# One more output tile kept in PSUM in the dense expert stage, and gates stored two first keys at a time

## The chip, the cores and the metric

The kernel runs on one core of a Trainium2 chip. The metric is the device time of one execution in microseconds. The engines are TensorE (PE, its weight loads PEld), VectorE (DVE), ScalarE (ACT), GpSimd (POOL), which here only issues gathers, and SyncE (SP), which issues all other DMAs.

## The reference

A decoder block on 1,024 tokens of width 1,024: RWKV-7 mixing beside differential attention, a gated merge, then a PEER layer of 16,384 experts, and a last RMSNorm. Only the PEER layer is touched by the change:

```python
q = (hf @ w_q).reshape(T, 8, 2, 128)
s = einsum('thcd,hcnd->thcn', q, sub_keys)      # 128 first keys, 128 second keys
v1, i1 = top_k(s[:, :, 0], 16); v2, i2 = top_k(s[:, :, 1], 16)
vals, ci = top_k((v1[..., :, None] + v2[..., None, :]).reshape(T, 8, 256), 16)
ids = first_key * 128 + second_key              # 8 x 16 experts of each token
gates = softmax(vals)
act = gelu(einsum('ced,cd->ce', u_tab[ids], x)) * gates
y = einsum('ce,ced->cd', act, v_tab[ids])
```

## The kernel before

The PEER layer is computed in two ways at the same time. Four blocks of 128 tokens take the **gather** way (`peer`, L809): for each of the 128 choices POOL gathers one row of `u`, and later one of `v`, for each token (128 x 1,024 floats, 512 KB, into one of NU = 5 buffers `uv`), and DVE does one instruction over 128x1024 on it (L817 for `u`, L824 for `v`). That makes 1,024 gathers and 1,024 long DVE instructions. A gather can start when DVE is done with the buffer that it takes.

The other 512 tokens take the **dense** way (`dense`, L864): all 16,384 experts as matrix products, one first key `e` (128 experts) at a time, with gates of 0 for the experts that a token did not choose. `head(e)` loads two tiles of `ut`, splits them in an upper and a lower part (`whi` on ACT, `wlo` on DVE), makes the dots with 24 matmuls in a PSUM bank `ua` of the pair `zbank` (L854), reads it out through Gelu on ACT (L886), multiplies by the gates on DVE (`gw`, L887), splits the result (`ah` on ACT, `al` on DVE), and loads and splits two tiles of `v` (`vh`, `vl`). Then each of eight output tiles (4 blocks of tokens x 2 halves of the width) gets three matmuls for this key. For e under NE = 16 the dots come from DRAM (`a_s`), where they were put during the gate stage.

PSUM has eight banks: `zbank` 2, `rbank` 3, `abank` 2, `obank` 1. Six of the output tiles are kept (`yk`) in the last three kinds for all 128 keys. The other two are moved: at every second key (CV = 2) `rest` (L902) makes the products of two keys, six matmuls, in a bank `yr` of `zbank`, and DVE adds it to `accd` in SBUF (L907). MV says ahead of which kept tile each `rest` stands: 0 and 3. The two `zbank`s go round over the dots and the two moved tiles.

The gate stage (`gates`, L827) comes just ahead. For 32 tokens at a time it builds gates in `st`, laid out as [second key, first key / CE, token, first key % CE], and writes them to DRAM (`gd_s`, L850). `dense` reads them back as `gt` (L882), CE = 4 first keys at a time, 512 tokens x 4 floats on a partition, in two buffers. So L887 reads one float of each group of four. At the end `finish` (L799) normalises each block: its square sums, the weight `fnw` loaded into a tile with the tag of `gt`, and the last product L806.

The order of the instructions on each engine is fixed before the run by the tile framework's planner. It goes by a clock of its own with its own costs: when an engine is free on that clock, the instruction that is ready and stands first in the program goes next. `dense` stands ahead of `peer` in the program, so its DVE instructions go first and the gathers' instructions fill what is left. On the chip each engine then runs its list strictly in order.

Of the kernel before, what the change touches and what calls it, by code (L numbers as in the profile page):

```python
# [8 lines left out]
F32 = mybir.dt.float32  # L9
# [9 lines left out]
P = 128  # L19
# [16 lines left out]
NE = 16  # L36
MV = (0, 3)
CHO = (1, 1, 1, 1, 0)
PADB = 8 * (16 * P + 16)
CE = 4  # L40
CV = 2
# [4 lines left out]
def body(ctx: ExitStack, tc: tile.TileContext, ins, out, dbg=None):  # L46
# [44 lines left out]

# [1 line left out]
    def const(name, shape, dt=F32):  # L93
# [57 lines left out]
    def wmul(o, src, xh, xl, n=8, step=1):  # L151
        """o = the sum over n [128, 128] parts of a weight tile src [n / 4, 128, 512], transposed, times xh(k) + xl(k).

        The lower parts of the weights come after the upper ones of step parts."""
        w = []
        for k0 in range(0, n, step):
            ks = range(k0, k0 + step)
            for k in ks:
                if k % 4 == 0:
                    w.append(wsplit(src[k // 4]))  # L160
                hi = w[-1][0][:, (k % 4) * P:(k % 4 + 1) * P]
                nc.tensor.matmul(o, hi, xh(k), start=(k == 0), stop=False)  # L162
                nc.tensor.matmul(o, hi, xl(k), start=False, stop=False)  # L163
            for k in ks:
                lo = w[k // 4][1][:, (k % 4) * P:(k % 4 + 1) * P]
                nc.tensor.matmul(o, lo, xh(k), start=False, stop=(k == n - 1))  # L166
# [10 lines left out]
    def invroot(ssq, n, scale, eps, op1=OP.add, pool=None):  # L177
        """(ssq * scale + eps) ** -0.5 for [128, n] (op1 max: the larger of the two)."""
        w = (pool or hp).tile([P, 32], F32, name="rsw", bufs=2)
        x, y, t, xh = (w[:, 8 * i:8 * i + n] for i in range(4))  # L180
        nc.vector.tensor_scalar(x, ssq, scale, eps, op0=OP.mult, op1=op1)
        nc.vector.tensor_scalar(xh, x, -0.5, None, op0=OP.mult)
        # a first guess from the exponent, then Newton's steps
        nc.vector.tensor_single_scalar(y.bitcast(U32), x.bitcast(U32), 1, op=OP.logical_shift_right)
        nc.vector.tensor_scalar(y.bitcast(U32), y.bitcast(U32), -1.0, 1597463007.0, op0=OP.mult, op1=OP.add)
        for _ in range(3):
            nc.vector.tensor_tensor(t, y, y, op=OP.mult)
            nc.vector.tensor_tensor(t, t, xh, op=OP.mult)
            nc.vector.scalar_tensor_tensor(y, t, 1.5, y, op0=OP.add, op1=OP.mult)
        return y  # L190
# [9 lines left out]
    def normed(src, w):  # L200
        """RMSNorm of rows of src, w over all partitions (two halves [128, 512] each)."""
        xn = [rt("xn") for _ in HALVES]
        ssq = tiny("ssq", 2)
        for i in range(2):
            nc.scalar.activation(xn[i], src[i], AF.Square, accum_out=ssq[:, i:i + 1])
        nc.vector.tensor_tensor(ssq[:, 0:1], ssq[:, 0:1], ssq[:, 1:2], op=OP.add)
        r = invroot(ssq[:, 0:1], 1, 1.0 / D, 1e-6)
        for i in range(2):
            nc.vector.scalar_tensor_tensor(xn[i], src[i], r[:, 0:1], w[i], op0=OP.mult, op1=OP.mult)
        return xn  # L210

    def to_cols(xn, a, hi, lo):
        """Rows of 128 tokens (two halves) to the transposed hi, lo [128, column / 128, token]."""
        o = slice(a * P, (a + 1) * P)
        for i in range(2):
            b = abank("tr")
            for k in range(4):
                nc.tensor.transpose(b[:, k * P:(k + 1) * P], xn[i][:, k * P:(k + 1) * P], ident)
            ks = slice(4 * i, 4 * i + 4)
            nc.scalar.activation(hi[:, ks, o], v4(b), AF.Copy)  # L220
            nc.vector.tensor_tensor(lo[:, ks, o], v4(b), hi[:, ks, o].bitcast(F32), op=OP.subtract)

    def head_stats(sq, W, scale, eps, op1):
        """Per token and half of the partitions: (sum(sq) * scale, eps) ** -0.5, spread back over them."""
        n = W // P
# [4 lines left out]
        o = rbank("hb")  # L230
# [7 lines left out]
    def mix(gi, t0, W):  # L238
# [27 lines left out]

# [1 line left out]
        c3 = lambda ap: ap.rearrange("p (c s) -> p c s", s=CH)  # L268
# [5 lines left out]
        def rwkv(h, kz, rz, vz):  # L274
# [46 lines left out]

            # A matrices, all transposed ([s, t]) and block diagonal over the chunks
            MB = [[None] * TT, [None] * TT]
# [36 lines left out]

            # (1 + A)^-1: blocks of 16 by substitution, a block to a partition, then doubling
            ab = gp.tile([64, 16, 16], F32, name="ab16", bufs=1)
# [73 lines left out]
            Pd, Qm = [], []  # L436
            # the state after a chunk is G * (Pd S + Qm): Pd with the 1, G already in Qm; off the heads' blocks 0
            def block(name, b, x, op):
# [67 lines left out]

# [1 line left out]
        def att_in(h):  # L508
# [20 lines left out]
        def attention(h, qT, kT, vn):  # L529
# [9 lines left out]
            for a in range(TT):  # L539
# [24 lines left out]
                if t0:  # L564
                    # the sums divide in the transposes: products with diagonal matrices
                    dg = at("dg")
# [61 lines left out]

# [1 line left out]
        yh, yl, mcat = [], [], []  # L630
# [50 lines left out]
    def pick(t0, W, fh, fl):  # L681
        """PEER: queries, keys, choice."""
        TT = W // P
# [30 lines left out]
    def choose(v1, i1, bi, last):  # L714
        """The 16 best sums of the two lists of each head: ids and gates [128, 128]."""
        cand = t4("cand")[:, :8 * NCAND].rearrange("p (h j) -> p h j", h=8)
# [23 lines left out]
        nc.vector.tensor_tensor(g3, g3, gsum[:, :, None].to_broadcast([P, 8, 16]), op=OP.mult)  # L740
        # position -> (i, j): the regions of REG hold 2^4, 2^3, 2^2, 2^1 columns
        d1, d2 = at("d1"), at("d2")
# [11 lines left out]
        nc.vector.tensor_tensor(fj, pf, ir, op=OP.subtract)  # L754
        # first row of a region less its first position >> its shift: 0, -2, -8, -24
        nc.vector.scalar_tensor_tensor(g1, h2, 2.5, g1, op0=OP.mult, op1=OP.add)
# [21 lines left out]
        if last:  # L778
            # with the choices over the partitions
            b = abank("sl")  # L780
# [18 lines left out]
    def finish(acc, rows, pool, tag, bufs):  # L799
        """The last norm of acc [128, 1024], and out."""  # L800
        ssq = pool.tile([P, 1], F32, name="ssqf", bufs=2)
# [7 lines left out]
    def peer(bi, ids, gate):  # L809
        """The chosen experts of 128 tokens, a choice at a time by gathers."""  # L810
        rows = slice(bi * P, (bi + 1) * P)
# [15 lines left out]
    def gates(sp, a, sl, eye8):  # L827
        """Gates [first key / CE, second key, token, first key % CE]: sums of outer products of one-hot rows."""
        e1, g = sl[:, 0:P], sl[:, 2 * P:3 * P]
# [27 lines left out]
    def ahead(sp, W, fh, fl, es):  # L857
        """The products with the rows of u of the first keys es, to a_s."""
        for e in es:
            t = sp.tile([P, 512], F32, name="ue", bufs=2)[:, :W]  # L860
            nc.scalar.activation(t, dots(e, W, fh, fl), AF.Copy)
            nc.sync.dma_start(ins["a_s"][e, :, 0:W], t)

    def dense(t0, W, fh, fl):  # L864
        """The experts of W tokens as matrix products over all of them, with gates of 0 for those not chosen."""
        TT = W // P
# [5 lines left out]
        outs = [(a, 0) for a in range(TT)] + [(a, 1) for a in range(TT)][::-1]  # L872
        banks = (rbank, rbank, rbank, obank, abank, abank)
        kept = {o: f("yk") for o, f in zip(outs, banks)}
# [3 lines left out]
        def head(e):  # L878
            """For the experts of first key e: weights (hi, lo: [128 second keys, W]), rows of v (hi, lo by halves)."""
            if e % CE == 0:  # L880
                gt[0] = fp.tile([P, 512, CE], F32, name="gt", bufs=2)
                nc.sync.dma_start(gt[0][:, :W], ins["gd_s"][e // CE, :, 0:W, :])  # L882
# [39 lines left out]
        for a in range(TT):  # L922
            for h in range(2):
                if (a, h) in kept:
                    y = acc[a][:, HALVES[h]]
                    nc.vector.tensor_tensor(y, y, kept[a, h], op=OP.add)
            finish(acc[a], slice(t0 + a * P, t0 + (a + 1) * P), fp, "gt", 2)

# [29 lines left out]
def prepare(inputs):  # L958
# [5 lines left out]
    a["x"] = c(g["x"].reshape(T, D))  # L964
    # [column tile, half of the rows, 128 rows, 4 row tiles x 128 columns]
    wt = lambda w: c(w.reshape(2, 4, P, -1, P).transpose(3, 0, 2, 1, 4).reshape(-1, 2, P, 512))
# [16 lines left out]
    a["lora"] = c(np.stack([np.concatenate([g["w2"][0], g["a2"][0]], axis=0), g["g2"][0]], axis=1))  # L983
    # constants of the shapes
    a["ident"] = np.eye(P, dtype=f)
# [45 lines left out]
```

## Time and profile before

| | |
|---|---|
| median of 3 runs | 3668.87 us (3668.75 to 3677.71) |
| profiled execution, span from first to last instruction | 3659.9 us |
| the median less that span (what lies around it) | 9.0 us |
| PE busy, DVE busy, ACT busy, POOL busy | 88%, 82%, 37%, 37% |
| DMA, mean over the span | 247 GB/s |

For the profiled execution its span is what is shown; a change in the span is taken as a change in the time. Busy shares are over the whole span, and the stages differ: from about 2290 to 3600 us PE, DVE and the DMA engines are all above nine tenths.

### The profile page before, as it was taken

How to read it: one execution, taken by the hardware profiler on the slowest of the kernel's cores; microseconds unless marked ns; L12 is line 12 of the kernel's file. 1: busy time of each engine (PE TensorE's matmuls, PEld its weight loads, DVE VectorE, ACT ScalarE, POOL GpSimd, SP SyncE). 2: the span in 40 equal slices, each digit the busy share in tenths (PEclk: the TensorE clock that was granted, in tenths of full speed). 3: DMA queues.
4: the chain of work that ended last, by engine and by line, in shares of the span. 5: the costliest groups of instructions: out<-in, count | busy, mean ns of one | idle time of the engine just before them, and what ended most of it. 6: DMA issues, size and time to landing. Idle time of an engine off the chain costs nothing. (4 is left out here: it accounts for less than half of the span.)

```text
span 3659.9 us, 46805 instructions
## 1 busy us (share of the span) xinstructions
PE 3224.0 (88%) x15166; PEld 2571.2 (70%) x15166; DVE 2995.0 (82%) x6666; ACT 1344.7 (37%) x2497; POOL 1350.5 (37%) x1100
## 2 busy tenths in 40 slices
PE   6999989998979796678888868999999999999997
PEld 5878867776857675556665656777777777777775
DVE  4655555978889888899988758998999999999997
ACT  3333433343323342122498863322222332222332
POOL 0000000004454445552012223656566665565652
PEclk9988989997979897788989879999999999999998
DMA  4222234426676667886467888999999999999995
GB/s 138 62 72 76 73 109 152 135 79 221 226 239 231 229 235 271 314 319 207 125 207 225 263 282 316 348 340 351 349 356 351 350 351 345 347 340 352 348 351 184
DMA packets 407110, 903.24 MB, mean 247 GB/s; under 512 B 52240, under 2 KB 139088, under 8 KB 402768
## 3 DMA queue, kind: packets, MB, share of 16 engines
q0 software_dynamic: 147456, 536.94, 41.6%
q1 hardware_dynamic: 259408, 363.31, 29.3%
q8 instruction: 119, 1.95, 0.2%
q14 instruction: 127, 1.04, 0.1%
HBM read 831.41 MB, written 68.69 MB: 246 GB/s over the span
## 5 line engine op out<-in xcount | busy, mean ns | idle before, releaser
L795 POOL DMA_INDIRECT uv<-u,ids x512 | 656.7, 1283 | 1140.4 <-DVE uv L817 538.3
L795 POOL DMA_INDIRECT uv<-v,ids x512 | 673.0, 1315 | 582.4 <-DVE acc L824 416.0
L824 DVE SCALAR_TENSOR_TENSOR acc<-uv,act,acc 128x1024 f32<-128x1024 f32 x512 | 655.9, 1281 | 52.4 <-DMA uv<-v,ids 46.0
L817 DVE SCALAR_TENSOR_TENSOR uv<-uv,hb 128x1024 f32<-128x1024 f32 x512 | 617.3, 1219 | 78.2 <-DMA uv<-u,ids 77.2
L147 ACT ACTIVATE whi<-wraw 128x512 fp32r<-128x512 f32 x552 | 344.7, 630 | 741.8 <-PE z L163 252.7
L162 PE MATMUL ua<-fh,whi 128*128 128x512 f32 x1024 | 428.7, 419 | 83.4 <-DVE accd L907 68.2
L148 DVE TENSOR_TENSOR wlo<-wraw,whi 128x512 fp32r<-128x512 f32 x552 | 373.7, 686 | 155.0 <-ACT whi L147 151.3
L163 PE MATMUL ua<-fl,whi 128*128 128x512 f32 x1024 | 422.6, 413 | 0.0
L173 PE MATMUL yk<-vh,ah 128*128 128x512 f32 x768 | 304.3, 396 | 21.7 <-ACT ah L169 20.8
L174 PE MATMUL yk<-vl,ah 128*128 128x512 f32 x768 | 304.3, 396 | 10.8 <-DVE vl L170 10.8
L162 PEld LDWEIGHTS ua<-fh,whi 128*128 128x128 f32 x1024 | 204.5, 200 | 147.5 <-DVE accd L907 85.9
L169 ACT ACTIVATE ah<-gw 128x512 fp32r<-128x512 f32 x128 | 80.8, 631 | 614.0 <-DVE gw L887 614.0
L175 PE MATMUL yk<-vh,al 128*128 128x512 f32 x768 | 304.0, 396 | 0.0
L162 PE MATMUL z<-hh,whi 128*128 128x512 f32 x672 | 273.8, 408 | 1.5 <-ACT whi L147 0.9
L166 PE MATMUL ua<-fh,wlo 128*128 128x512 f32 x1024 | 266.6, 400 | 5.3 <-DVE wlo L148 5.3
L166 PE MATMUL z<-hh,wlo 128*128 128x512 f32 x672 | 270.7, 403 | 0.0
L163 PE MATMUL z<-hl,whi 128*128 128x512 f32 x672 | 270.0, 402 | 0.0
L846 PE MATMUL gb<-oh,ohg 128*128 128x128 f32 x1024 | 226.4, 342 | 40.5 <-ACT ohg L845 39.1
L846 PEld LDWEIGHTS gb<-oh,ohg 128*128 128x128 f32 x1024 | 166.1, 209 | 103.8 <-ACT ohg L845 66.5
L163 PEld LDWEIGHTS ua<-fl,whi 128*128 128x128 f32 x1024 | 204.4, 200 | 44.6
L166 PEld LDWEIGHTS ua<-fh,wlo 128*128 128x128 f32 x1024 | 195.0, 191 | 48.5 <-DVE wlo L148 5.8
L845 ACT ACTIVATE ohg<-ohb,sl 128x128 f32<-128x128 bf16 x512 | 228.1, 537 | 2.5 <-DVE ohb L840 2.4
(325 smaller groups left out, 6199.0 us busy)
## 6 DMA issues: line engine op xcount, KB each, us to landing
wraw<-ut SPq DMA_DIRECT2D x256, 256.0 KB, 6.4
vraw<-v SPq DMA_DIRECT2D x256, 256.0 KB, 6.5
wraw<-w_in SPq DMA_DIRECT2D x168, 256.0 KB, 2.7
gd_s<-st SPq DMA_DIRECT2D x16, 2048.0 KB, 11.2
gt<-gd_s SPq DMA_DIRECT2D x32, 1024.0 KB, 8.9
wraw<-wq SPq DMA_DIRECT2D x64, 256.0 KB, 2.9
g_s<-sgo SPq DMA_DIRECT2D x32, 256.0 KB, 3.1
wraw<-proj SPq DMA_DIRECT2D x32, 256.0 KB, 3.6
```

The lines of the kernel that those rows point to most:

```text
L147: nc.scalar.activation(hi, raw, AF.Copy)
L148: nc.vector.tensor_tensor(lo, raw, hi.bitcast(F32), op=OP.subtract)
L162: nc.tensor.matmul(o, hi, xh(k), start=(k == 0), stop=False)
L163: nc.tensor.matmul(o, hi, xl(k), start=False, stop=False)
L166: nc.tensor.matmul(o, lo, xh(k), start=False, stop=(k == n - 1))
L173: nc.tensor.matmul(o, ah, bh, start=first, stop=False)
L174: nc.tensor.matmul(o, ah, bl, start=False, stop=False)
L175: nc.tensor.matmul(o, al, bh, start=False, stop=last)
L795: nc.gpsimd.indirect_dma_start(out=t, out_offset=None, in_=ins[src], in_offset=bass.IndirectOffsetOnAxis(ap=ids[:, j:j + 1], axis=0))
L817: nc.vector.scalar_tensor_tensor(u, u, 1.0, hb, op0=OP.mult, op1=OP.mult, accum_out=act[:, j:j + 1])
L824: nc.vector.scalar_tensor_tensor(acc, v, act[:, j:j + 1], acc, op0=OP.mult, op1=OP.add)
L846: nc.tensor.matmul(b[:, k * P:(k + 1) * P], o3[:, k], o1[:, k], start=True, stop=True)
```

## The change

Seven output tiles are kept instead of six; the seventh takes one of the two `zbank`s. One tile is left to be moved, and its `rest` stands ahead of the third kept tile (MV = (2,)). The dots of all keys and this tile now share the one `zbank` that is left. CE goes from 4 to 2: `gd_s` is [64, 128, 512, 2] instead of [32, 128, 512, 4], `st` and `gt` follow, and `gt` has three buffers of half the size, which `finish` uses too. Comments and docstrings are dropped.

```diff
-MV = (0, 3)
+MV = (2,)
-CE = 4
+CE = 2
 def dense(t0, W, fh, fl):
-        banks = (rbank, rbank, rbank, obank, abank, abank)
+        banks = (rbank, rbank, rbank, obank, abank, abank, zbank)
 def head(e):
             if e % CE == 0:
-                gt[0] = fp.tile([P, 512, CE], F32, name="gt", bufs=2)
+                gt[0] = fp.tile([P, 512, CE], F32, name="gt", bufs=3)
                 nc.sync.dma_start(gt[0][:, :W], ins["gd_s"][e // CE, :, 0:W, :])
...
-            finish(acc[a], slice(t0 + a * P, t0 + (a + 1) * P), fp, "gt", 2)
+            finish(acc[a], slice(t0 + a * P, t0 + (a + 1) * P), fp, "gt", 3)
```

## Rows read from the trace of the kernel before

**Rows 1.** Busy time by stretch: PE, PEld, DVE, ACT, POOL, PEclk, DMA share, GB/s

```profile
1760.00:2180.00 420.00, 337.09 (x1490) 252.35 (x1488) 330.40 (x885) 330.89 (x723) 88.79 (x76) 0.89 0.70 219
2180.00:2289.00 109.00, 97.06 (x399) 75.28 (x400) 94.93 (x114) 39.25 (x69) 40.36 (x31) 0.98 0.89 322
2289.00:3604.40 1315.40, 1245.77 (x5221) 995.20 (x5220) 1227.81 (x1641) 382.33 (x659) 787.29 (x594) 0.98 0.95 347
3604.40:3637.90 33.50, 33.28 (x143) 26.44 (x142) 22.79 (x40) 6.45 (x11) 0.00 (x0) 1.00 0.13 47
```

**Rows 2.** The same columns: eight key pairs beside u, eight beside v

```profile
2553.70:2752.40 198.70, 184.88 (x771) 147.40 (x770) 183.11 (x302) 55.96 (x96) 120.70 (x94) 0.97 0.96 352
2800.30:2987.90 187.60, 181.31 (x772) 145.60 (x771) 179.38 (x198) 56.09 (x96) 114.77 (x86) 0.99 0.96 349
```

**Rows 3.** The same stretch by source line: L824, L817 (with accumulator reads), L887

```profile
2289.00:3604.40 1315.40, 433.31 (x338) 0.98 0.95 347
...
2289.00:3604.40 1315.40, 309.00 (x512) 0.98 0.95 347
...
2289.00:3604.40 1315.40, 117.90 (x109) 0.98 0.95 347
```

**Rows 4.** DVE's groups in those two stretches of eight pairs

```profile
L817 DVE SCALAR_TENSOR_TENSOR uv<-uv,hb 128x1024 f32<-128x1024 f32 x94 | 112.6, 1220 | 15.8 <-DMA uv<-u,ids 15.7
...
L824 DVE SCALAR_TENSOR_TENSOR acc<-uv,act,acc 128x1024 f32<-128x1024 f32 x85 | 108.9, 1281 | 8.2 <-DMA uv<-v,ids 7.0
...
L887 DVE TENSOR_TENSOR gw<-gw,gt 128x512 f32<-128x512 f32 x16 | 17.4, 1085 | 0.0
L907 DVE TENSOR_TENSOR accd<-accd,yr 128x512 f32<-128x512 f32 x16 | 10.8, 677 | 0.0
```

**Rows 5.** The waits from 2289 to 3604 us: total, times, longest

```profile
PE ua L162 <- DVE accd L907: 68.0, 36, 4.7
```

**Rows 6.** Timeline of one key pair: ACT, DVE, PE (start, duration, idle before)

```profile
2805.49 0.60 ACT L886 ACTIVATE gw<-ua 128x512 f32<-128x512 f32 x1 [1.19 <-PE ua L166]
...
2812.30 1.05 DVE L887 TENSOR_TENSOR gw<-gw,gt 128x512 f32<-128x512 f32 x1
2813.27 0.68 DVE L907 TENSOR_TENSOR accd<-accd,yr 128x512 f32<-128x512 f32 x1
...
2814.01 0.50 PE L162 MATMUL ua<-fh,whi 128*128 128x512 f32 x1 [1.56 <-DVE accd L907]
...
2824.90 1.07 DVE L887 TENSOR_TENSOR gw<-gw,gt 128x512 f32<-128x512 f32 x1
```

**Rows 7.** The DMA issues: KB each, median us to landing

```profile
wraw<-ut SPq DMA_DIRECT2D x256, 256.0 KB, 6.4
vraw<-v SPq DMA_DIRECT2D x256, 256.0 KB, 6.5
...
gt<-gd_s SPq DMA_DIRECT2D x32, 1024.0 KB, 8.9
```

**Rows 8.** The DMA queue 109.5 to 112.5 (64-byte runs), 2149 to 2153 us (512-byte)

```profile
q1 hardware_dynamic: 528, 0.03, 11.7%
...
q1 hardware_dynamic: 2267, 1.16, 102.8%
```

**Rows 9.** ACT's groups of the whole span: the gates' copy out, a plain copy out

```profile
L847 ACT ACTIVATE st<-gb 128x512 f32<-128x512 f32 x128 | 77.3, 604 | 2.6 <-PE gb L846 1.3
...
L699 ACT ACTIVATE psc<-s 128x512 f32<-128x512 f32 x32 | 19.2, 599 | 38.7 <-PE s L697 38.7
```

**Rows 10.** Timeline of the end: loads of fnw on SP, the last product

```profile
3640.06 1.36 SPq L804 DMA_DIRECT2D fnw<-fnw  x2
...
3646.20 0.33 SPq L804 DMA_DIRECT2D fnw<-fnw  x1
...
3653.91 1.29 DVE L806 SCALAR_TENSOR_TENSOR accd<-accd,rsw,fnw 128x1024 f32<-128x1024 f32 x1 [1.52 <-DMA fnw<-fnw]
```

**Rows 11.** Busy time by stretch: the two fastest pairs beside u

```profile
2704.60:2752.40 47.80, 45.16 (x195) 35.96 (x194) 45.83 (x78) 13.94 (x24) 29.55 (x24) 1.00 0.98 370
```

## The prediction

> **What bounds the kernel now.** I read the busy time by stretch first. The dense stage runs from about 2180 us to the last matmul at 3637.9, and in its long part DVE is 93% busy (1227.81 of 1315.40 us), PE 95%, the DMA engines 95% at 347 GB/s [rows 1]. Three resources look full, so the question is which one sets the pace. Second view: two stretches of eight key pairs that differ only in the gathers beside them. Beside `u` DVE is 92.2% busy (183.11 of 198.70), beside `v` 95.6% (179.38 of 187.60). If DVE set the pace it would be as full in both; what stays nearly the same is the rate, 352 against 349 GB/s [rows 2]. The time follows the bytes. A gather is 512 KB (0.524 MB), a pair loads four tiles of `ut` and four of `v` of 256 KB and half a `gt` of 1,024 KB [rows 7], 2.62 MB. With 94 and 85 gathers in eight pairs [rows 4] a pair moves 8.78 and 8.19 MB; over 24.84 and 23.45 us that is 353 and 349 GB/s. I conclude that the DMA engines pace this part, and that DVE follows with a few per cent to spare.
>
> Third, the waits. TensorE's wait for the moved tile's add is 68.0 us in all [rows 5], and looks like the prize. The timeline says why it exists: Gelu was read out at 2805.49 + 0.60, its gate product runs at 2812.30, 6 us later, because DVE works through its list late; the add stands just behind it and the next dots wait 1.56 us for the bank [rows 6]. TensorE waits because it is faster than the pace. It needs 96 matmuls a pair; without gathers 143 took 33.50 us [rows 1], so 0.234 us each and 22.5 us a pair, against 1315.40 us over 109 keys [rows 3], 24.1 us a pair.
>
> Last, the end: the last gather's product stands at 3604, and the dense part then runs alone for 33.5 us with the DMA engines at 13% [rows 1]. The work after it is free of gathers; where the gathers end on the list decides the length of that piece.
>
> **The change part by part.** *Seventh tile kept.* The matmuls are the same in number: a moved tile costs six in two keys, a kept one three and three. DVE loses one add a pair, 0.677 us [rows 4], less one last add. Kept at nothing directly, because DVE doesn't set the pace; what it does is in the next two items.
>
> *The list is packed anew.* Gathers' products fill what dense leaves free on the planner's clock. Eight pairs hold 94 products of `u` but 85 of `v` [rows 4], so the list is full on DVE's side there: a limit of POOL or of buffers would give the two the same count. With 0.677 us freed and 1.281 us a product, 0.53 more products go into a pair. There are 338 + 512/2 = 594 products in 54.5 pairs [rows 3], 10.9 a pair; at 11.43 they are through in 52.0 pairs. So 2.5 pairs fewer run beside gathers, and 2.5 more behind them. Beside the gathers that saves 2.5 x 2.62 MB = 6.55 MB, 19 us at 347 GB/s; behind them the pairs cost 2.5 x 22.5 = 56 us. Net **+37 us**. If the planner's clock doesn't repack it is 0; if it also counts a faster gate product (below) up to 1.48 us is freed, 1.16 products, and by the same sum about +78. I take the removed add alone.
>
> *Gate product.* L887 takes 1085 ns where it picks one float of each 16 bytes, against 677 for the add without gaps [rows 4]. With CE = 2 it picks one of each 8. No row shows that stride: between 0 and 0.4 us saved a key; I take the middle, 0.2, since neither end is nearer, so 0.4 a pair. The Trainium skill's page SBUF — State Buffer, section Door 1: The DMA port swizzle, says that accesses run at full rate with two or more hits in each 16-byte line. By it the whole 0.4 us a key is saved, DVE falls by another 0.4 us a pair, and the sum below would come out some 5 us lower.
>
> *A lighter DVE.* A pair has 22.5 us of DVE now; less 0.68 and 0.4, plus 0.53 x 1.281 = 0.68, gives 22.1 us over (11.43 x 0.524 + 2.62) / 0.347 = 24.8 us: 89% instead of 93%. By the two stretches above, 3.4 points less DVE went with 0.9% more bytes per second, so 4 points give 1.1% of the some 1,297 us left: **-14 us**. Bounds: nothing, and the best stretch seen, share 0.98 against 0.95 [rows 11], 3%, -39.
>
> *One bank for dots and moved tile.* `rest` now waits for Gelu: two kept tiles, six matmuls or 1.4 us, cover its 0.60 us. The add must be done within five kept tiles, 3.5 us, and DVE is about 6 us late, so TensorE waits for it at every pair; the matmuls behind it wait too. That costs nothing as long as DVE doesn't in turn wait for the dots: from the add's end at 2813.95 to the next gate product at 2824.90 are 10.95 us, and the dots (24 x 0.234 = 5.6) and Gelu need about 6.5. The cover is 4.4 us; the add stands further behind in the list by one or two instructions, up to 2.6 us. If the cover is gone, each further microsecond costs one a pair.
>
> *Gates to DRAM.* The same bytes in runs of 256 bytes instead of 512: 131,072 packets for 65,536. 528 packets of about 60 bytes took 11.7% of 3 us of 16 engines, 10.6 ns each; 2,267 of 512 bytes 102.8% of 4 us, 29 ns [rows 8]. A straight line gives 18.5 ns for 256 bytes, so 131,072 x 18.5 / 16 = 152 us of all engines for 119: 33 more in a stage of 420 us at 0.70 [rows 1], hidden behind ACT at 79%. I take +3. Bound above: 29 ns each, 119 us more, share 0.98, about +10. The copy out to `st` writes runs of 16 bytes at 604 ns, as fast as a plain one (599) [rows 9]; with 8-byte runs I take 0, bound 0.4 x 128 = 51 us on ACT. The Trainium skill's page DMA: Bandwidth & Descriptors, section Specifications, wants 512 bytes for full rate and names a read-modify-write below; by it the upper end holds, and the rows of 60-byte packets speak against it.
>
> *gt.* 32 loads more on SP's list, each half as big, in three buffers: a buffer is free after the same key as before, so nothing behind them on SP waits longer. The first lands earlier, between nothing and 2.5 us (8.9 against 6.5 for 256 KB [rows 7]): **-1**.
>
> *The end.* `finish` had two `fnw` tiles, so four blocks go in two rounds: loads at 3640.06, and again from 3646.20, last product at 3653.91 [rows 10]. With three, blocks that are ready early load ahead and one is left for the second round: **-4** (0 to -6).
>
> Sum: +37 - 14 + 3 - 1 - 4 = +21. On the span 3659.9 + 21 = 3681; with the 9.0 us around it about **3689 us**, 0.5% slower.
>
> **The rivals.** *A, not repacked:* as many products a pair as before. Then DVE has 21.4 us a pair over 24.1, 89%, the same 1.1%, and the sum is -14 + 3 - 1 - 4 = -16, **3653**. For it: no row shows the planner's clock. Against it: the two counts. This is the other side.
>
> *B, DVE sets the pace after all:* repacked, and the DMA engines climb to 0.98 or full. Then +37 - 39 - 2 = -4, **3665**; at full share (5%, -65) -30, **3639**. For it: DVE at 93% is nearly full too [rows 1]. Against it: the two rates that are nearly one.
>
> *C, the shared bank:* the add falls so far behind that the cover of 4.4 us is gone. One microsecond a pair over 54 pairs: +54, **3743**.
>
> *D, dear gates:* short runs cost as much as long ones (+10 for +3), or the copy out slows (+51): **3696 to 3740**.
>
> **How the numbers follow.** 0.3% is 11 us, about what a measurement of this kernel can tell from no change. Chances: forecast 0.48 (0.38 slower, 0.10 within), A 0.20 (0.16 faster, 0.04 within), B 0.21 (0.11 faster, 0.10 within), C 0.05, D 0.06. So faster 0.27, same 0.24, slower 0.49. The forecast's own range is 3670 to 3705 by the bounds of the DMA rate and of the gate product. Over all: low end at B's far end, 3640, below A; high end takes in D's near end and no gain of rate, 3714. C and the far ends are left out.
>
> **What would show it.** Right: about 11.4 products a pair instead of 10.9, the last one on the list some five keys earlier, a piece at the end without gathers of about 90 us instead of 33.5, 350 GB/s before it; L887 well under 1.08 us; TensorE's wait for `accd` longer in all, no wait of L887 for Gelu in the long part. Wrong: the same number of products a pair (A), 360 GB/s and more (B), L887 waiting for L886 at every pair (C), a gate stage longer than 420 us (D).

## The result: 0.8% slower, inside the range

The changed kernel takes 3696.03 us in the median of 4 runs (3692.94 to 3699.85), the kernel before 3668.81 us beside it (4 runs, 3664.74 to 3677.71): a ratio of 1.0079, 95% interval 1.0061 to 1.0097. Forecast were 3689 us, a range of 3640 to 3714, and "slower" at 0.49 as the likeliest of three. The profiled span is 3698.1 us. A few executions of the experiments below were slower by several per cent with the same kernel; the ratios leave them out, the medians hold them.

First the busy time by stretch of the changed kernel, in the columns of [rows 1]. The second line is the gap between the gates and the first gate product, the fourth the stretch with gathers up to the last gather's product, the fifth what the dense part then does alone, the last the end.

```profile
1760.00:2180.00 420.00, 343.19 (x1490) 260.41 (x1489) 335.88 (x890) 332.16 (x720) 95.54 (x82) 0.86 0.77 216
2180.00:2197.00 17.00, 0.00 (x0) 0.00 (x0) 8.31 (x7) 0.33 (x1) 6.14 (x7) 0.50 1.03 406
2197.00:2308.40 111.40, 98.93 (x385) 77.01 (x386) 91.55 (x113) 40.62 (x71) 43.23 (x35) 0.91 0.95 336
2308.40:3565.20 1256.80, 1173.23 (x4888) 935.49 (x4887) 1116.61 (x1529) 365.46 (x616) 744.82 (x577) 0.97 0.96 352
3565.20:3678.70 113.50, 113.50 (x490) 91.58 (x488) 45.72 (x80) 32.90 (x54) 0.00 (x0) 1.00 0.23 73
3678.70:3698.10 19.40, 0.04 (x1) 0.00 (x0) 11.56 (x57) 4.38 (x8) 0.00 (x0) 0.63 0.58 216
```

The slowdown stands in the fifth line. For 113.5 us TensorE is busy without a gap, POOL does nothing and the DMA engines are at 23%: dense key pairs without gathers beside them. Before, that piece was short [rows 1]. The same stretch with gathers, by source line (L824, L817 with its accumulator reads, L887), answers [rows 3]:

```profile
2308.40:3565.20 1256.80, 416.18 (x325) 0.97 0.96 352
...
2308.40:3565.20 1256.80, 309.33 (x512) 0.97 0.96 352
...
2308.40:3565.20 1256.80, 70.75 (x102) 0.97 0.96 352
```

These are 325 + 256 = 581 products in 102 keys, 51 pairs: 11.39 products a pair, where [rows 3] gave 10.9. Eight pairs beside `u` and eight beside `v`, as in [rows 2]:

```profile
2528.70:2732.10 203.40, 184.96 (x764) 147.10 (x763) 178.60 (x302) 56.92 (x97) 124.58 (x98) 0.97 0.97 354
2805.70:2994.80 189.10, 181.01 (x768) 144.25 (x767) 173.84 (x194) 56.87 (x96) 117.43 (x89) 0.99 0.97 357
```

Eight pairs take 203.4 and 189.1 us instead of 198.7 and 187.6, though DVE has become emptier (87.8% and 91.9% instead of 92.2% and 95.6%): the list is fuller. DVE's groups in these two stretches, as in [rows 4]:

```profile
L817 DVE SCALAR_TENSOR_TENSOR uv<-uv,hb 128x1024 f32<-128x1024 f32 x98 | 117.7, 1220 | 24.8 <-DMA uv<-u,ids 24.4
...
L824 DVE SCALAR_TENSOR_TENSOR acc<-uv,act,acc 128x1024 f32<-128x1024 f32 x89 | 113.9, 1280 | 15.0 <-DMA uv<-v,ids 13.8
...
L887 DVE TENSOR_TENSOR gw<-gw,gt 128x512 f32<-128x512 f32 x17 | 11.9, 701 | 0.0
L907 DVE TENSOR_TENSOR accd<-accd,yr 128x512 f32<-128x512 f32 x8 | 5.4, 674 | 0.0
```

Four products more are done in eight pairs (98 and 89 for 94 and 85), and DVE waits longer for the gathers (24.4 and 13.8 us for 15.7 and 7.0). The gate product takes 701 ns for 1085; the add stands there once a pair instead of twice. The waits from 2308.4 to 3565.2 us (total, times, longest), as in [rows 5]:

```profile
PEld ua L162 <- DVE accd L907: 103.2, 45, 5.4
PE ua L162 <- DVE accd L907: 83.6, 45, 5.0
DVE uv L817 <- DMA uv<-u,ids: 71.1, 85, 2.6
...
DVE acc L824 <- DMA uv<-v,ids: 58.2, 85, 2.1
...
DVE gw L887 <- ACT gw L886: 0.5, 2, 0.3
```

TensorE's wait for the moved tile's add has grown from 68.0 [rows 5] to 83.6 us; L887 waited 0.5 us in all for Gelu.

**Where the 38 us of span are.** Four pieces, each after less before. The first gate product starts at 2197.33 us instead of 2177.83: +19.5. From there to the end of the last gather's product it takes 1367.9 instead of 1433.7 us (to 3565.2, and before to 3611.5): -65.8. From there to the last matmul 113.5 instead of 26.4: +87.1. The end 19.4 instead of 22.0: -2.6. Sum +38.2. The lines of before that these readings rest on (the first gate product and the last gather's product in DVE's timeline; the end by stretch, in the columns of [rows 1]):

```profile
2177.83 1.06 DVE L887 TENSOR_TENSOR gw<-gw,gt 128x512 f32<-128x512 f32 x1 [4.57 <-ACT gw L886]
...
3610.23 1.28 DVE L824 SCALAR_TENSOR_TENSOR acc<-uv,act,acc 128x1024 f32<-128x1024 f32 x1
...
3637.90:3659.90 22.00, 0.23 (x1) 0.00 (x0) 12.15 (x57) 4.49 (x8) 0.00 (x0) 0.57 0.52 191
```

And the first gate product after:

```profile
2197.33 0.69 DVE L887 TENSOR_TENSOR gw<-gw,gt 128x512 f32<-128x512 f32 x1 [5.90 <-ACT gw L886]
```

The times differ by 27 us only. The profiled execution after took 3699.85 us, 1.8 more than its span and 3.8 more than the median, and in all later profiles the time was 1.7 to 1.9 us above the span as well. The 9.0 us that the prediction added for before therefore hold a profiled execution about 7 us faster than the median.

### The profile page after: what moved, and what is told of

It is laid out like the page before. It is cut to its first block, busy times and chain, and to the rows that moved or that the text cites. A ratio compares the mean times of both kernels' runs of the same rounds, so it can differ in the third digit from the quotient of the medians.

```text
span 3698.1 us, 46867 instructions
## 1 busy us (share of the span) xinstructions
PE 3228.4 (87%) x15166; PEld 2580.6 (70%) x15166; DVE 2915.7 (79%) x6603; ACT 1356.9 (37%) x2497; POOL 1319.5 (36%) x1100
## 5 line engine op out<-in xcount | busy, mean ns | idle before, releaser
L795 POOL DMA_INDIRECT uv<-u,ids x512 | 642.5, 1255 | 1130.2 <-DVE uv L817 513.1
L795 POOL DMA_INDIRECT uv<-v,ids x512 | 656.3, 1282 | 575.7 <-DVE acc L824 402.6
L824 DVE SCALAR_TENSOR_TENSOR acc<-uv,act,acc 128x1024 f32<-128x1024 f32 x512 | 655.3, 1280 | 90.1 <-DMA uv<-v,ids 83.6
L817 DVE SCALAR_TENSOR_TENSOR uv<-uv,hb 128x1024 f32<-128x1024 f32 x512 | 617.0, 1218 | 95.7 <-DMA uv<-u,ids 94.3
L148 DVE TENSOR_TENSOR wlo<-wraw,whi 128x512 fp32r<-128x512 f32 x552 | 374.1, 686 | 192.5 <-ACT whi L147 140.9
L173 PE MATMUL yk<-vh,ah 128*128 128x512 f32 x896 | 355.9, 398 | 24.6 <-DMA gw<-a_s 24.1
L174 PE MATMUL yk<-vl,ah 128*128 128x512 f32 x896 | 355.7, 397 | 5.4 <-DVE vl L170 5.4
L175 PE MATMUL yk<-vh,al 128*128 128x512 f32 x896 | 355.2, 396 | 0.0
L173 PEld LDWEIGHTS yk<-vh,ah 128*128 128x128 f32 x896 | 169.3, 189 | 66.3 <-ACT ah L169 24.6
```

What stands on the lines that cost most here:

```text
L148: nc.vector.tensor_tensor(lo, raw, hi.bitcast(F32), op=OP.subtract)
L173: nc.tensor.matmul(o, ah, bh, start=first, stop=False)
L174: nc.tensor.matmul(o, ah, bl, start=False, stop=False)
L175: nc.tensor.matmul(o, al, bh, start=False, stop=last)
L795: nc.gpsimd.indirect_dma_start(out=t, out_offset=None, in_=ins[src], in_offset=bass.IndirectOffsetOnAxis(ap=ids[:, j:j + 1], axis=0))
L817: nc.vector.scalar_tensor_tensor(u, u, 1.0, hb, op0=OP.mult, op1=OP.mult, accum_out=act[:, j:j + 1])
```

## The experiments

All were timed in five rounds beside the kernel before; a ratio is to it, with a 95% interval. The expectations count products and keys on the planner's list, where the kernel before has 11.0 products a pair and the whole change 11.55; the results count them in the traces, which give 10.9 and 11.39. The theory (T1): time freed on DVE lets the planner's list take in more products a pair, the gathers end earlier, and the dense pairs left over run alone. Its rivals: the copying of gates in short runs (T2), and the shared bank (T3).

**e1, the seventh tile alone.**

```diff
 # before
-MV = (0, 3)
+MV = (2,)
...
-        banks = (rbank, rbank, rbank, obank, abank, abank)
+        banks = (rbank, rbank, rbank, obank, abank, abank, zbank)
```

> Seventh tile kept and one zbank, but gates four first keys at a time as before. The instruction list has 8 keys left behind the last gather's product (2 before the change, 10 with the whole change). Theory 1, the list (a key that runs behind the gathers costs 11.2 us of TensorE, beside them 3.8 us of DMA, so 7.5 us for each one moved): 6 x 7.5 = 45, less some 8 for a lighter DVE, about 3706. Theory 2, the gates and their small runs are what costs: as before, 3669. Theory 3, the bank that dots and moved tile share: as the whole change, 3696.

Measured: 3710.7 us, 1.0129 (1.0107 to 1.0152). The tile alone costs 46 us, more than the whole change. Its trace has 11.4 products a pair (593 in 104 keys), and eight keys stand behind the last product. Busy time of its stretch with gathers and of the piece behind it:

```profile
2292.30:3588.00 1295.70, 1197.56 (x4978) 954.42 (x4977) 1177.46 (x1556) 371.56 (x629) 790.48 (x591) 0.97 0.96 348
3588.00:3678.60 90.60, 90.56 (x391) 72.96 (x389) 39.96 (x67) 24.43 (x41) 0.00 (x0) 1.00 0.19 58
```

The lone piece is 90.6 us; the rate is 348 GB/s, as before. The gates play no part here, and the first gate product starts at 2177.7 us, as before.

**e2, the gates alone.**

```diff
 # before
-CE = 4
+CE = 2
...
-                gt[0] = fp.tile([P, 512, CE], F32, name="gt", bufs=2)
+                gt[0] = fp.tile([P, 512, CE], F32, name="gt", bufs=3)
...
-            finish(acc[a], slice(t0 + a * P, t0 + (a + 1) * P), fp, "gt", 2)
+            finish(acc[a], slice(t0 + a * P, t0 + (a + 1) * P), fp, "gt", 3)
```

> Gates two first keys at a time, but six tiles kept and two zbanks as before. The list has 4 keys left behind the last gather's product. Theory 1, the list: 2 x 7.5 = 15, less some 12 for the faster gate product and 4 at the end: within a few us of before, 3668. Theory 2, the gates: 3696. Theory 3, the bank: as before, 3669.

Measured: 3653.34 us, 0.997 (0.9956 to 0.9984), faster, and 15 us better than T1 itself said. T2 falls. The busy time of the same two stretches:

```profile
2303.30:3573.40 1270.10, 1213.66 (x5148) 969.99 (x5147) 1171.29 (x1624) 375.69 (x650) 729.99 (x582) 0.99 0.97 355
3573.40:3623.50 50.10, 50.06 (x216) 40.15 (x214) 24.16 (x46) 12.47 (x21) 0.00 (x0) 1.00 0.09 32
```

The 54 pairs of the first line take 23.5 us each, against 1315.40 / 54.5 = 24.1 [rows 1, 3], at 10.8 products a pair. The list was not packed denser for the cheaper gate product, and the rate rose to 355 GB/s. Not all of that is shown to come from a lighter DVE: e9 below has the same cheap gate product without the short runs, and reached 351.

**e3 and e4, DVE filled again.** If freed time on DVE does the damage, useless work that takes it up again should help.

```diff
 # after
+        fill = fp.tile([P, 512], F32, name="fill", bufs=1)
+        nc.vector.memset(fill, 0.0)
...
             nc.vector.tensor_tensor(w, w, gt[0][:, :W, e % CE], op=OP.mult)
+            if e % 2 == 0:      # e4: at every key
+                nc.vector.tensor_tensor(fill, w, fill, op=OP.max)
```

> The whole change, and in every key pair one more DVE instruction of 128x512 (a maximum of the gated result into a tile that nobody reads): DVE does more, and the planner leaves room for fewer gathers' products beside a pair; 5 keys are left behind the last one instead of 10. Theory 1, the list: 5 x 7.5 = 37 us faster than the whole change, 3659. Theories 2 and 3: not faster than the whole change, 3696 or more, since only work is added.

Measured: 3662.8 us, 0.9993 (0.998 to 1.0007). An instruction of 0.69 us whose result nobody reads, 64 times on DVE, makes the changed kernel 33 us faster. The list is back at 10.8 products a pair (585 in 108 keys) with five keys behind the last one:

```profile
2322.50:3596.50 1274.00, 1219.61 (x5135) 975.86 (x5135) 1171.74 (x1620) 383.15 (x647) 737.99 (x581) 0.98 0.96 354
3596.50:3651.30 54.80, 54.38 (x234) 43.39 (x232) 26.08 (x50) 13.63 (x23) 0.00 (x0) 1.00 0.10 34
```

> The whole change, and one such DVE instruction more in every key; no key is left behind the last gather's product. Theory 1, the list: up to 10 x 7.5 = 75 us faster than the whole change, less what the gathers now take behind the last key; about 3636, faster than the kernel before. Theories 2 and 3: 3696 or more.

Measured: 3663.07 us, 0.9994 (0.9979 to 1.0008), no further gain, and the 3636 expected fell. At 10.4 products a pair the balance has tipped over:

```profile
2316.60:3639.80 1323.20, 1270.61 (x5369) 1015.84 (x5367) 1225.12 (x1706) 395.27 (x668) 750.53 (x583) 0.99 0.95 341
3639.80:3668.70 28.90, 0.05 (x1) 0.00 (x0) 21.31 (x81) 5.53 (x10) 2.86 (x2) 0.59 0.69 241
```

The last matmul is now at 3639.8, but the last product comes behind it, as the timeline of DVE shows (start, duration, wait):

```profile
3652.47 1.28 DVE L824 SCALAR_TENSOR_TENSOR acc<-uv,act,acc 128x1024 f32<-128x1024 f32 x1 [2.79 <-DMA uv<-v,ids]
```

Now the gathers end last, 14 us behind the dense part, and the rate has fallen to 341 GB/s. The order in which the two streams end is what the filler moves.

**e5, the moved tile ahead of the sixth kept tile instead of the third.** The add then has less time to free the shared bank.

```diff
 # after
-MV = (2,)
+MV = (5,)
```

> The whole change with the moved tile ahead of the sixth kept tile instead of the third, so that two kept tiles (1.4 us) instead of five (3.5 us) stand between its matmuls and the next dots in the same bank. The list has 10 keys left behind the last gather's product, as with the whole change. Theory 1, the list: no difference from the whole change, 3696. Theory 3, the shared bank: 2.1 us more at each of 56 pairs, 115 us, about 3810.

Measured: 3690.82 us, 1.0063 (1.0042 to 1.0083), no slower than the whole change. TensorE's wait for the add is 73.6 us in the stretch with gathers. T3 falls.

**e6 and e10, fewer bytes.** The prediction held that the DMA engines pace the long part; here the second half of the rows of `v` is loaded once instead of at every key, 0.52 MB less of the 2.62 MB that a pair loads [rows 7].

```diff
 # before (e6), after (e10)
+        v1 = fp.tile([P, 512], F32, name="v1raw", bufs=1)
+        nc.sync.dma_start(v1, ins["v"][0:P, HALVES[1]])
...
-                raw = fp.tile([P, 512], F32, name="vraw", bufs=NVR)
-                nc.sync.dma_start(raw, ins["v"][e * P:(e + 1) * P, c])
+                raw = v1
+                if h == 0:
+                    raw = fp.tile([P, 512], F32, name="vraw", bufs=NVR - 1)
+                    nc.sync.dma_start(raw, ins["v"][e * P:(e + 1) * P, c])
```

> The kernel before, but the second half of the rows of v is loaded for the first key only and that tile is used for all keys: 0.52 MB of 8.2 to 8.8 MB less a pair, every instruction of TensorE, VectorE and ScalarE as before, and the same list (11.0 products a pair, 2 keys behind the last). If the DMA engines pace the long part: 6% less a pair, down to TensorE's 22.5 us, some 70 us faster, 3595. If VectorE paces it: no change, 3665.

Measured: 3647.7 us, 0.9964 (0.9946 to 0.9981). Some 15 us of the 70 expected. The busy time of its stretch with gathers:

```profile
2294.80:3605.00 1310.20, 1243.41 (x5247) 992.46 (x5246) 1232.73 (x1648) 383.52 (x663) 787.80 (x593) 0.99 0.92 326
```

The rate fell to 326 GB/s and the share of the DMA engines to 0.92, with DVE at 94% (1232.73 of 1310.20). They had room, so they do not pace this part by themselves.

> The whole change, and the second half of the rows of v loaded once, as in e6: 0.52 MB less a pair, the list as with the whole change (11.55 products a pair, 10 keys behind the last). If VectorE, a lighter one here, no longer paces the long part and the DMA engines do: up to 6% of 1,257 us, some 60 us faster than the whole change, 3636. If VectorE still paces it as in e6: 15 us faster, 3681.

Measured: 3681.95 us, 1.0042 (1.0026 to 1.0059): 14 us less than the whole change, the same as in e6, though DVE was at 90% in its stretch with gathers:

```profile
2303.10:3535.80 1232.70, 1160.72 (x4864) 926.26 (x4863) 1113.50 (x1528) 364.83 (x615) 748.04 (x576) 0.98 0.94 336
```

The emptier DVE did not make the bytes the bound.

**e9, the gate product reads its gates without gaps.** In the kernel before, so that only L887's duration changes and nothing in the gate stage; the gates that it reads are those of other tokens and keys.

```diff
 # before
-            nc.vector.tensor_tensor(w, w, gt[0][:, :W, e % CE], op=OP.mult)
+            nc.vector.tensor_tensor(w, w, gt[0].rearrange("p t f -> p (t f)")[:, e % CE * W:(e % CE + 1) * W], op=OP.mult)
```

> The kernel before, but the gate product reads 512 floats in a row from the gate tile instead of one of each four (other values, the same loads): VectorE has 0.40 us less a key, 0.8 us a pair, and the list, the loads and the two banks stay as they were (11.0 products a pair, 2 keys behind the last). If VectorE paces the long part: up to 0.8 x 55 pairs = 44 us faster, 3620. If the DMA engines pace it, as the prediction had it: 3.3 points less VectorE, 0.9% more bytes a second, 12 us, 3651.

Measured: 3642.28 us, 0.9942 (0.9925 to 0.996), between the two. L887 takes 695 ns, 0.39 us less, 50 us over 128 keys; some 21 us of them come back. The busy time of its stretch with gathers:

```profile
2290.20:3594.40 1304.20, 1241.98 (x5248) 993.73 (x5247) 1194.30 (x1650) 383.51 (x662) 750.58 (x594) 0.99 0.96 351
```

A 91.6% busy DVE gave 351 GB/s. The list kept 10.9 products a pair (597 in 110 keys) and two keys behind the last.

**e11, four gather buffers.** If neither DVE nor the DMA engines pace alone, the round of a buffer may: POOL issues into a free one, the gather lands, DVE reads it.

```diff
 # before
-NU = 5
+NU = 4
```

> The kernel before with four buffers for gathered rows instead of five. The list has 11.0 products a pair as before, 1 key behind the last (2 before) and 5 products fewer ahead of the first gate product. e6 and e9 left open what sets the rest of the pace, since less VectorE gave half of its worth and fewer bytes a fifth. If the way round of a buffer (issue, some 7 us to landing, the product) sets it: the 11 us of a buffer's round with five allow one gather in 2.2 us, with four one in 2.8, about 25% of the long part, +300 us, 3970. If VectorE and the DMA engines pace it between them: within 20 us of before, 3665.

Measured: 3785.6 us, 1.0331 (1.0309 to 1.0352): between the two again. DVE's groups of the two products over the whole span, e11:

```profile
L824 DVE SCALAR_TENSOR_TENSOR acc<-uv,act,acc 128x1024 f32<-128x1024 f32 x512 | 655.9, 1281 | 140.2 <-DMA uv<-v,ids 134.7 <-DVE wlo L148 0.4
L817 DVE SCALAR_TENSOR_TENSOR uv<-uv,hb 128x1024 f32<-128x1024 f32 x512 | 619.2, 1219 | 142.3 <-DMA uv<-u,ids 141.0
```

The same view of before:

```profile
L824 DVE SCALAR_TENSOR_TENSOR acc<-uv,act,acc 128x1024 f32<-128x1024 f32 x512 | 655.9, 1281 | 52.4 <-DMA uv<-v,ids 46.0
L817 DVE SCALAR_TENSOR_TENSOR uv<-uv,hb 128x1024 f32<-128x1024 f32 x512 | 617.3, 1219 | 78.2 <-DMA uv<-u,ids 77.2
```

DVE waits 276 us for gathers in all, against 123 us before. Six buffers weren't tried.

**e7 and e8, a better version.** e2 with its lone piece of 50 us has a DVE a little too light for the list, and ACT is far from full. So the upper part `ah` of the weights moves from ACT to DVE, at every fourth key (e7) or every second (e8).

```diff
 # e2
-            split(w, ah, al)
+            if e % 2 == 0:      # e7: e % 4 == 0
+                nc.vector.tensor_copy(ah, w)
+                nc.vector.tensor_tensor(al, w, ah.bitcast(F32), op=OP.subtract)
+            else:
+                split(w, ah, al)
```

> Gates two first keys at a time, six tiles kept as before, and for every fourth key the upper part of the gated dots is rounded on VectorE instead of ScalarE. The list has 3 keys left behind the last product, 4 in the kernel without it. Theory 1, the list: 7 us faster than that, about 3646. Theories 2 and 3: not faster than 3653.

Measured: 3637.45 us, 0.9923 (0.9902 to 0.9943).

> The same for every second key. The list has 2 keys left. Theory 1, the list: 2 x 7.5 = 15 us faster than gates alone, less a little for a busier VectorE, about 3640, faster than the kernel before by 25. Theories 2 and 3: not faster than 3653.

Measured: 3632.1 us, 0.9905 (0.9885 to 0.9925), faster than both kernels, and 8 us better than expected. Busy time of its two stretches:

```profile
2310.90:3587.90 1277.00, 1241.72 (x5279) 995.14 (x5278) 1204.04 (x1698) 360.79 (x608) 724.98 (x583) 0.99 0.97 354
3587.90:3606.90 19.00, 19.00 (x83) 15.01 (x81) 12.86 (x29) 3.02 (x5) 0.00 (x0) 1.00 0.15 55
```

The moved instruction in DVE's groups over the whole span:

```profile
L891 DVE CAST ah<-gw 128x512 fp32r<-128x512 f32 x64 | 28.9, 452 | 0.0
```

The moved cast adds 28.9 us to DVE, and yet the kernel is faster: 10.6 products go into a pair (587 in 111 keys), two keys stand behind the last one, and 354 GB/s stay, with DVE at 94% of its stretch. The lone piece is 31 us shorter than in e2, 1.4 pairs; at 15 us for a pair moved back beside the gathers (two keys at 7.5 us) that makes the 21 us measured. This version keeps six tiles.

**e12, one key less ahead in the gate stage.** Meant to undo the late start of the dense stage.

```diff
 # after
-NE = 16
+NE = 15
```

> The whole change with NE = 15: one first key less has its dots made in the gate stage, the dense stage makes them itself (24 matmuls, 5.6 us of TensorE more in it). On TensorE's list two groups of dots instead of four then stand between the last gate matmul and the first kept tile, 397 products instead of 407 stand ahead of the first gate product on DVE's list, and as many products a pair as in the whole change. If the late start of the dense stage (its first gate product 19.5 us later than before) is a loss of its own: the first gate product some 15 to 20 us earlier, 10 products more among the pairs, so one pair of 22.5 us less behind the gathers, and the whole some 10 us faster after the 5.6 us, 3686. If the late start costs nothing, since the 12 products made in it are not made later: 3696 to 3702, the dots added.

Measured: 3689.47 us, 1.006 (1.0046 to 1.0074). In the profiled execution, the slowest of the six, the first gate product stands at 2199.56 us. The gates' last matmul ended at 2151.5 us there, 9.5 us later than in the changed kernel, so from the one to the other are 48.0 us instead of 55.3 (31.4 before). Three groups of dots stood between them instead of the two expected, and 404 products ahead of the first gate product instead of 397; ten keys were left behind the gathers as with the whole change. The edit did little of what it was meant to, so the run does not tell the two apart.

## Why the forecast held, and where its sizes were off

**The list is packed anew: right, and shown.** 11.39 products a pair where 11.43 were forecast. e1 has the effect without the gates, e3 takes it away by work that nobody needs, and e8 turns it into a gain. The lone piece was forecast at about 90 us: e1 measures 90.6, the whole change 113.5. That e1 agrees is luck: the forecast was 33.5 + 56 us, where the first measured 26.4 (next paragraph) and the second 64. The last product stands eight keys earlier than before (ten keys left for two), where five were forecast. Rival A is out.

**The term +37 was too small.** 490 matmuls at 96 a pair [rows 1] are 5.1 pairs alone; before it was 26.4 us, 1.2 pairs (the last gather's product ended at 3611.5, not at 3604 as the prediction read it). So 3.9 pairs lost their gathers instead of 2.5, and by the prediction's own sum, 22.5 less 7.5 us a pair, that is 59 us for 37. The denser list by itself is in e1: 90.6 less 26.4 us, 2.9 pairs, or three by its eight keys for two; at 15 us a pair 43 to 45 us, and e1 lost 46. About one more pair comes from a step that was not foreseen, the next one.

**The hand-over from the gates: not foreseen.** The prediction gave the gates +3 and the first `gt` -1. The last gate matmul ended at 2142.0 us, earlier than before (2146.4), and yet the dense stage began 19.5 us later. It comes with the gates: e1 without them starts at 2177.7 us, e2 with them alone at 2197.7. SP's waits between 2140 and 2200 us in the changed kernel:

```profile
SPq L850 <- ACT st L847: 16.6, 1, 16.6
SPq L144 <- DVE wlo L148: 15.9, 5, 5.6
SPq L144 <- DMA wraw<-ut: 7.3, 1, 7.3
SPq L882 <- DMA a_s<-ue: 5.1, 1, 5.1
```

And the second of them in the kernel before:

```profile
SPq L144 <- DVE wlo L148: 1.0, 2, 0.8
```

Behind the last gate matmul the planner put four groups of dots of `ahead`, before it was two. SP's loads of `wraw` for them wait for DVE to be through with earlier tiles (L148), and DVE's list has gathers' products between those; `gt` and the first `vraw` stand behind on SP. That this chain is what delays the start is read from the order of the lists; no run tests it. In that time 407 products were done ahead of the first gate product instead of 395, which is the one more pair that ends up alone. What the late start costs was not isolated: e2 is faster than before in spite of it.

**A lighter DVE: -14 came near, but not by its rule.** With all of the change the rate went from 347 to 352 GB/s, 1.4%, some 18 us. The gain goes with the gate product and not with the add: e9, the cheap gate product alone, reached 351 GB/s, e1, one add a pair less, 348. e9 gained 21 us for 0.39 us a key, where the term's rule of thumb (3.4 points of DVE for 0.9%; 0.78 us a pair are 3.2 points) gives 11; in e2 the pairs became 0.6 us shorter. Nor does the rate follow DVE's busy share, as the rule has it: e8 had 354 GB/s with DVE at 94%, e1 348 at 91%. What the rate does follow stays open.

**The gate product.** The middle value, 0.2 us a key, was wrong: L887 fell from 1085 to about 695 ns, and e9's reading without gaps takes the same 695 ns. So one float of each 8 bytes costs nothing here, one of each 16 bytes 0.39 us an instruction. This agrees with the Trainium skill's page SBUF — State Buffer, section Door 1: The DMA port swizzle, which wants two or more hits in a line of 16 bytes for the full rate.

**"The DMA engines pace this part, and DVE follows": too strong.** This is the step that failed. e6 took away a fifth of the dense part's bytes and got a fifth of their time back (15 of 70 us); e9 took DVE time away and got less than half; e11 took a buffer away and lost 120 us, less than the round alone would cost. The runs fit a loop of five buffers that goes over POOL, the DMA engines and DVE, in which each link gives only part of what it saves; that none of the three links changed sets the pace alone is shown; how the loop shares it out is argued, and that the links take turns in setting the pace would fit these runs as well. TensorE is not far off either: a pair takes 23.0 us in e8, and its matmuls need 22.5. Rival B (3639 to 3665) did not come true either, since the rate stayed at 352.

**The shared bank: right.** It costs nothing, by e5 and by the 0.5 us that L887 waited for Gelu. TensorE's longer wait (83.6 us) lies inside the pace. Rival C is out.

**Gates to DRAM: right on the price.** The DMA queue of the changed kernel from 2148 to 2152 us, in the last write of `gd_s`, as in [rows 8]:

```profile
q1 hardware_dynamic: 3372, 0.86, 104.8%
```

Two of its DMA issues over the whole span (KB each, median us to landing), as in [rows 7]:

```profile
gd_s<-st SPq DMA_DIRECT2D x16, 2048.0 KB, 13.5
gt<-gd_s SPq DMA_DIRECT2D x64, 512.0 KB, 7.5
```

By the queue, 1.048 x 4 us x 16 engines / 3372 packets is 19.9 ns each, where 18.5 were estimated and 29 was the bound. The Trainium skill's page DMA: Bandwidth & Descriptors, section Specifications, wants 512 bytes for full rate. The queue moved 0.86 MB in these 4 us, against 1.16 MB with 512 bytes [rows 8]: it was slower, as the page has it, but by a quarter and not by the half of the bound. The DMA share of the gate stage rose from 0.70 to 0.77, and its last matmul came no later. The copy out to `st` stayed at its price (609 ns a time, 604 before). Rival D is out at its prices; the late start is another cost of the gates, which it did not name.

**The end: -2.6 for -4.** Three loads of `fnw` went out at once and one later; the last product waits 1.33 us for it.

Put together on the span: +59 for +37, -18 for -14, -2.6 for -4 make +38, which is what was measured, for +21 forecast; beside the one more pair alone, the late start leaves nothing in this sum, which is an account and not a test of it. The time came 7 us above the forecast only, where the span came 17 us above: the 9.0 us around the span were 1.8, and the profiled execution was 3.8 us above its median. That closeness is luck.

## What to carry to other kernels

Where a planner fills a nearly full engine's list from a second stream of work, time freed on that engine is not a gain by itself: it moves the second stream forward, and what was hidden beside it stands alone at the end. Read where each stream ends before and after, count the filler's instructions per round of the main loop, and aim at both ending together; here a worthless instruction or a moved cast set that balance better than a saved add. And an engine that is 95% busy is not yet the one that sets the pace: take away bytes, work and buffers one at a time and see how much of each comes back.

## What the runs showed of the hardware that was not expected

DVE's cast of a 128x512 tile to the split's upper part takes 452 ns (e8), where ACT's activation for the same tile took 632 ns (e9's group of `ah`). Packets of 256 bytes took 19.9 ns each, and 0.86 MB of them went in 4 us, 216 GB/s; packets of 512 bytes took 29 ns, and 1.16 MB went in 4 us, 290 GB/s [rows 8]. With four gather buffers instead of five a gather landed sooner (median 6.2 and 6.6 us for 7.1), and the kernel was still 3.3% slower.
